# A two-layer transformer block on one core: the second layer's output projection in a new order, its splits and low parts moved

## The chip, the core and the metric

The kernel runs on one core of a Trainium2 chip. Its engines have queues of their own and wait for each other by semaphores: TensorE (PE, matrix products out of SBUF into PSUM; PEld is its weight load), VectorE (DVE), ScalarE (ACT), GpSimd (POOL) and SyncE (SP, which here issues most DMAs). Every queue is worked off in the order in which the program wrote it. The metric is the device time of one execution in microseconds, the median of several runs.

## What is computed

Two layers of a diffusion transformer on 256 latent tokens (x) and 256 context tokens, width 1024: a half FFN, an attention with three branches, a second half FFN; both halves and the attention are modulated by vectors made from a condition. In the second layer the context ends with the attention, so that all behind it is 256 tokens wide. The change concerns the lines marked by the arrows, for the second layer:

```python
def _half_ffn(h, g, shift, scale, gate, w_up, w_down):
    return h + 0.5 * gate * _swiglu(_modulate(_rmsnorm(h, g), shift, scale), w_up, w_down)
...
        o_a = _neighbourhood_attn(q_a, k_a, v_a, k_a_c, v_a_c, na_rpb[l])
        o_b = _pool_mix(p_x[..., OFF_B_U:OFF_C_Q], pool_w[l], pool_scale[l])
        o_c = _gqa_blocks(q_c, jnp.concatenate([k_c, k_c_c], axis=1), jnp.concatenate([v_c, v_c_c], axis=1))
        h_x = h_x + mod_x[:, :, 5] * (jnp.concatenate([o_a, o_b, o_c], axis=-1) @ w_out[l])      # <-
        h_x = _half_ffn(h_x, norm_g[l, 2], mod_x[:, :, 6], mod_x[:, :, 7], mod_x[:, :, 8], ffn2_up[l], ffn2_down[l])   # <-
```

## The kernel before

**Layout.** The residual stream hT lies transposed in SBUF: 8 chunks of 128 features by 512 columns, the first 256 of them x. All weights come from HBM as float32 and every product is made of three: an operand is split into a high part (rounded to the type fp32r) and a low part (the rest), and mm3 (L345) adds high x high, high x low and low x high in PSUM (L349, L350, L351; L644 to L646 in the last FFN).

**Weights.** They come as a stream in the order of use. SP loads 1 MB at a time into one of three raw buffers (loads, L167). A raw buffer is split into two slots by emit_split (L292): ACT makes the high part (L307), DVE the low part by a subtraction (L310); 128 x 1024 for each here. There are seven slot buffers, used also for attention's keys and transposed probabilities. st["out"] counts the slots that are split and not yet used up; pump (L328) splits ahead while it is under st["look"]; take hands the next slot out (and splits it, if that hasn't been done) and done gives it back and pumps. A raw buffer is free for its next load when both its splits are done.

**Order.** The program is written out by hand for each queue. A clock counted along with the matmuls (tick) fires what was put off by later(us, ...): adds, statistics, pumps.

**The stretch in question.** At the end of the second layer's attention, the last two head pairs (1 and 3 of the four of the third branch, L1010 to L1023: a product, the spread of the sums, then ACT's high part L1022 and DVE's low part L1023) are computed after all others. Then st["look"] becomes 5 at once and 6 some 6 us of the counted clock later (LOOKS), so three slots are split in a row. w_out_phase (L1198) calls proj_out (L468) for the second half of w_out, the third branch's 512 features: eight chunks of 128 output features, four steps of 128 input features each (one step a head pair). The weight is four slots of two chunks each. The first two slots are taken one after the other, with two PSUM banks each, and the steps go 0, 1, 2, 3; each slot given back lets pump split another. The last two slots are taken together and their four chunks done one by one. PSUM has five banks for such products (ps_mm).

After each chunk comes resid (L463, DVE: PSUM times the gate plus hT), then plain_operand's chunk (L610): with chunk 0 a memset and two small operations on the operand's last columns (L614, L615, L616), then for each chunk ACT's high part of hT times the norm's gain (L619) and DVE's low part (L620). Then acc_chunk (L364): ACT squares the chunk (L372, L375) and POOL adds the squares (L382), put off by 2.3 us of the counted clock. After the last chunk, after (L629) puts off the norm's statistics (stat, L404: matmuls L411, then a chain of small operations on DVE from L390 to L399) by 3.6 and the factors (L418, L625) by 6.6; a pump follows at 4.5 (REFILL).

last_ffn (L634) doesn't wait for the statistics: it multiplies the operand without the norm's factor, which is applied to the products afterwards (L662 to L675). Its product 0 needs one chunk of the operand for each of its eight steps, product 1 the same chunks with the next slot, and so on; f0, f1, f2, ... are the slots of these products. proj_out also calls ada_step (L196) after each of the first two slots, for the modulation vectors; when the second layer's projection runs, none are left to be made.

Of the kernel before, what the change touches and what calls it, by code (L numbers as in the profile page):

```python
# [18 lines left out]
TX = 256  # L19
# [7 lines left out]
RAW_BUFS = 3  # L27
NA_LOOK = (5, 5)
GQA_LOOK = (4, 3)
LOOKS = (((0, 5), (3.0, 6)), ((0, 5), (6.0, 6)))  # L30
ADAQ = lambda nc: nc.sync
ADA_AHEAD = 2
AT = ((1, 2), (0, 1), (0, 1))
# [18 lines left out]
def dit_kernel(  # L52
# [50 lines left out]
    def later(us, fn):  # L103
        pending.append([clock[0] + us, fn])
# [184 lines left out]
            return True  # L289
        return False  # L290

    def emit_split(between=None):  # L292

        if not next_main(True):
            tick(0.0)
            assert next_main(True)
        i, j = st["split"], st.get("sub", 0)
        _, src, shape, splits = stream[i]
        raw = slots[("raw", i)]
        a, b = shape  # L300
        v = raw[:, 0:a * b].rearrange("p (a b) -> p a b", a=a)
        sl = splits[j](v)
        n0, n1 = sl.shape[1], sl.shape[2]
        w = wp.tile([128, 2, 1024], F32R, tag="w", name="w")
        wh = w[:, 0, 0:n0 * n1].rearrange("p (a b) -> p a b", a=n0)
        wl = w[:, 1, 0:n0 * n1].rearrange("p (a b) -> p a b", a=n0)
        ACT.copy(out=wh, in_=sl)  # L307
        if between:
            between()
        DVE.tensor_tensor(out=wl, in0=sl, in1=wh.bitcast(F32), op=ALU.subtract)  # L310
        slots[("w", st["nslot"])] = (wh, wl)
        st["nslot"] += 1
        st["out"] += 1
        j += 1
        if j == len(splits):
            slots.pop(("raw", i))
            if i not in borrowed:
                st["raws"] -= 1
            i, j = i + 1, 0
            loads()  # L320
        st["split"], st["sub"] = i, j
# [23 lines left out]
    def mm3(ps, pairs, n, start, stop):  # L345

        last = len(pairs) - 1
        for i, ((wh, wl), (ah, al)) in enumerate(pairs):
            PE.matmul(out=ps, lhsT=wh, rhs=ah, start=start and i == 0, stop=False)  # L349
            PE.matmul(out=ps, lhsT=wh, rhs=al, start=False, stop=False)  # L350
            PE.matmul(out=ps, lhsT=wl, rhs=ah, start=False, stop=stop and i == last)  # L351
            tick(3 * MM[n])

    def wcol(slot, k, j):
        return slot[0][:, k, j * 128:(j + 1) * 128], slot[1][:, k, j * 128:(j + 1) * 128]

    def acol(a, k, lo, hi):
        return a[:, 0, k, lo:hi], a[:, 1, k, lo:hi]
# [5 lines left out]
    def acc_chunk(vs, k):  # L364

        lo, hi = vs[0] * TX, vs[-1] * TX + TX
        if k == 0:
            if 0 in vs:
                accs["sum"] = tmp.tile([128, NT], F32, tag="acc", bufs=1, name="acc")
            for v in vs:  # L370
                accs[v] = [accs["sum"][:, v * TX:v * TX + TX]]
            ACT.activation(out=accs["sum"][:, lo:hi], in_=hT[:, k, lo:hi], func=AF.Square)  # L372
            return
        sq = tmp.tile([128, NT], F32, tag="t2k", bufs=T2K, name="sq")[:, 0:hi - lo]
        ACT.activation(out=sq, in_=hT[:, k, lo:hi], func=AF.Square)  # L375
        if k == KD - 1:
            for v in vs:
                accs[v].append(sq[:, v * TX - lo:v * TX - lo + TX])
        else:
            acc = accs["sum"]  # L380
            eng = POOL if st["ends"] == 4 else DVE
            adds.append(lambda: eng.tensor_tensor(out=acc[:, lo:hi], in0=acc[:, lo:hi], in1=sq, op=ALU.add))  # L382
            later(ACC_LAG[st["ends"]], lambda: adds and adds.pop(0)())
# [77 lines left out]
    def resid(ps, k, v, gate):  # L461
        cols = slice(v * TX, v * TX + TX)
        DVE.scalar_tensor_tensor(out=hT[:, k, cols], in0=ps, scalar=gate[:, k, v:v + 1], in1=hT[:, k, cols], op0=ALU.mult, op1=ALU.add)  # L463
# [4 lines left out]
    def proj_out(src, kl, ppair, gate, both, final, after, each=None, first=None):  # L468


        n = NT if both else TX
        nsl = KD // ppair
        for i in range(nsl - 2 if final else nsl):
            s = take()
            pss = [mm_bank() for _ in range(ppair)]
            for k in range(kl):
                for j in range(ppair):
                    mm3(pss[j][:, 0:n], [(wcol(s, k, j), src(k, 0, n))], n, k == 0, k == kl - 1)
            for j in range(ppair):
                for v in halves(both):  # L480
                    resid(pss[j][:, v * TX:v * TX + TX], ppair * i + j, v, gate)
                if final:
                    if first:
                        first(ppair * i + j)
                    acc_chunk(halves(both), ppair * i + j)
                    if each:
                        each(ppair * i + j)
            done()
            ada_step()
        if not final:  # L490
            return
        sl = [take() for _ in range(2)]
        for v in halves(both):
            for i in range(2):
                for j in range(ppair):
                    ch = ppair * (nsl - 2 + i) + j
                    ps = mm_bank()
                    mm3(ps[:, 0:TX], [(wcol(sl[i], k, j), src(k, v * TX, v * TX + TX)) for k in range(kl)], TX, True, True)
                    resid(ps[:, 0:TX], ch, v, gate)
                    if first:  # L500
                        first(ch)
                    acc_chunk((v,), ch)
                    if each:
                        each(ch)
            after(v)
        st["out"] -= 2
        later(REFILL[st["ends"]], pump)
        st["ends"] += 1
# [94 lines left out]
    def plain_operand(i):  # L603


        l, n = divmod(i, 3)
        shift = modT[:, l * 72 + 3 * n * 8:l * 72 + 3 * n * 8 + 8, 0:1]
        a = {"wait": []}

        def chunk(k):  # L610
            if k == 0:
                t = actp.tile([128, 8192], F32R, tag="act", name="act")[:, 0:2 * KD * NX]
                a["t"] = t = t.rearrange("p (s k t) -> p s k t", s=2, k=KD)
                DVE.memset(t[:, :, :, TX + 1:NX].bitcast(F32), 0.0)  # L614
                ACT.copy(out=t[:, 0, :, TX:TX + 1], in_=shift)  # L615
                DVE.tensor_tensor(out=t[:, 1, :, TX:TX + 1], in0=shift, in1=t[:, 0, :, TX:TX + 1].bitcast(F32), op=ALU.subtract)  # L616
            ah, al = acol(a["t"], k, 0, TX)
            g = gsc[:, i, k, 0:1]
            ACT.activation(out=ah, in_=hT[:, k, 0:TX], func=AF.Copy, scale=g)  # L619
            DVE.scalar_tensor_tensor(out=al, in0=hT[:, k, 0:TX], scalar=g, in1=ah.bitcast(F32), op0=ALU.mult, op1=ALU.subtract)  # L620

        def factors():
            rb = spread(0)
            a["rb"] = tmp.tile([128, NT], F32, tag="acc", bufs=1, name="rb")[:, 0:TX]
            ACT.copy(out=a["rb"], in_=rb[:, 0:TX])  # L625
            while a["wait"]:
                a["wait"].pop(0)()

        def after(v):  # L629
            later(3.6, lambda: stat(0))  # L630
            later(6.6, factors)
        return a, chunk, after
# [564 lines left out]

    def w_out_phase(l, O, both, after, first=None):  # L1198
        gate = modT[:, l * 72 + 40:l * 72 + 48, :]
        proj_out(lambda k, lo, hi: acol(O, 4 + k, lo, hi), 4, 2, gate, both, True, after, None, first)  # L1200


    ada_all = [[(g, k) for k in range(KD)] for g in range(9)]
# [7 lines left out]
    with tc.manual_schedule():  # L1211
# [100 lines left out]
        def first():  # L1312

            ps = [mm_bank() for _ in range(4)]

            def dense(h, js):
                for k in (2 * h, 2 * h + 1):
                    for j in js:
                        mm3(ps[j], [(wcol(sl[j], k, 0), acol(a["t"], k, 0, NT))], NT, k == 0, k == KD - 1)
            sl = [take() for _ in range(4)]  # L1320
            for h in range(3):
                dense(h, range(0, AT[h][0]))
                sb = quarter_ada(h + 1)
                if h == 0:
                    raws.append(quarter_load(3, 1, fresh()))
                else:
                    st["raws"] -= 1
                    loads()
                dense(h, range(AT[h][0], AT[h][1]))
                quarter_finish(h + 1, sb)  # L1330
                dense(h, range(AT[h][1], 4))
            st["raws"] -= 1
            loads()
            for i in range(2):
                dense(3, (2 * i, 2 * i + 1))
                done(2)
            return ps
# [117 lines left out]
```

## Time and profile before

| | us |
|---|---|
| runs | 1714.87, 1713.21, 1712.35 |
| median | 1713.21 |
| profiled execution | 1716.47 |
| its span | 1714.7 |

The span is the time between the first and the last instruction of the profiled execution; durations and starts below are counted from its beginning. A time in the profile is of that one execution, not of the median. The kernel's line numbers are those in the profile: "PE mm L349" is the matmul of line 349. For the stretch in question one reads the waits of an engine (who waited for whom, us in total, times, longest), the order of time of each engine (start, duration, what ran, in brackets the idle time before it and what ended it), and stretches of equal length with each engine's busy time and the clock granted to PE. Where instructions with the same text follow each other, a row merges them and gives their count.

### The profile page before, as it was taken

What the parts mean: (1) busy time and instruction counts of PE and PEld (TensorE: products, weight loads), DVE (VectorE), ACT (ScalarE), POOL (GpSimd) and SP (SyncE); (2) the same over time, 40 slices, a digit from 0 to 9 for tenths busy, and PEclk for the clock granted to TensorE, in tenths of its full rate; (3) what the DMA queues carried; (4) which work ended last, traced back from release to release, by engine and by line L of the source; (5) the groups of instructions that cost most, each with busy time, mean ns of one, the idle gap of its engine ahead of it and who ended that gap; (6) DMA issues with size and microseconds to landing.
All of it is one profiled execution on the core that took longest, in us unless ns stands there. A gap on an engine that the chain in (4) does not pass through costs nothing.

```text
span 1714.7 us, 23726 instructions
## 1 busy us (share of the span) xinstructions
PE 1679.2 (98%) x9512; PEld 1421.6 (83%) x9512; DVE 1037.6 (61%) x1782; ACT 670.8 (39%) x1135; POOL 43.6 (3%) x66
## 2 busy tenths in 40 slices
PE   6999999999999999999999999999999999999998
PEld 4778888889886798888888898888888987789998
DVE  4666577667555676666764466545433656676674
ACT  4432222334556644222233243213222356654443
POOL 0000200000010000000000000020000000000000
PEclk8999999999999999999999999999999999999999
DMA  9745556431304325554553335455532234555561
GB/s 314 203 165 174 166 164 190 163 131 51 111 25 172 108 72 177 172 154 136 172 171 118 98 87 182 145 155 174 151 99 88 66 111 148 172 172 175 169 199 50
DMA packets 295335, 246.48 MB, mean 144 GB/s; under 512 B 9377, under 2 KB 262442, under 8 KB 293176
## 3 DMA queue, kind: packets, MB, share of 16 engines
q1 hardware_dynamic: 292680, 241.30, 45.5%
q0 software_dynamic: 1088, 2.15, 0.5%
q8 instruction: 75, 1.23, 0.3%
q10 hardware_dynamic: 1456, 1.52, 0.3%
q14 instruction: 36, 0.29, 0.1%
HBM read 243.88 MB, written 2.00 MB: 143 GB/s over the span
## 4 chain that ended last, share of the span: by engine, by line
PE 89%; DVE 4%; DMA 3%; ACT 2%; issue 1%; SPq 0%; DVEq 0%; ACTq 0%
PE mm L349 25%; PE mm L350 24%; PE mm L351 24%; PE mm L644 2%; PE mm L645 2%; PE mm L646 2%; PE mm L1010 1%; DVE w L310 1%; PE aux L976 1%; DMA ada_raw<-in_w_ada_dram 1%; PE ada L182 1%; PE mm L936 1%; DVE ada_acc L222 1%; PE mm L937 1%; PE ada L230 1%
## 5 line engine op out<-in xcount | busy, mean ns | idle before, releaser
L349 PE MATMUL mm<-act,w 128*128 128x512 f32 (+1 forms) x2240 | 810.8, 362 | 4.5 <-ACT act L1022 2.2
L350 PE MATMUL mm<-act,w 128*128 128x512 f32 (+1 forms) x2240 | 804.0, 359 | 1.1 <-DVE act L433 0.9
L351 PE MATMUL mm<-act,w 128*128 128x512 f32 (+1 forms) x2240 | 803.3, 359 | 1.7 <-DVE w L310 1.7
L310 DVE TENSOR_TENSOR w<-raw,w 128x1024 fp32r<-128x1024 f32 (+1 forms) x312 | 371.3, 1199 | 220.2 <-ACT w L307 219.2
L349 PEld LDWEIGHTS mm<-act,w 128*128 128x128 f32 x2240 | 424.9, 190 | 86.0 <-issue 15.9
L351 PEld LDWEIGHTS mm<-act,w 128*128 128x128 f32 x2240 | 424.8, 190 | 64.6 <-DVE w L310 2.5
L350 PEld LDWEIGHTS mm<-act,w 128*128 128x128 f32 x2240 | 425.0, 190 | 62.9 <-DVE act L433 1.4
L307 ACT CAST w<-raw 128x1024 fp32r<-128x1024 f32 (+1 forms) x312 | 315.4, 1025 | 119.9 <-PE mm L351 92.7
L222 DVE SCALAR_TENSOR_TENSOR ada_acc<-ada_raw,sc,ada_acc 128x512 f32<-128x512 f32 x308 | 216.2, 747 | 51.2 <-DMA ada_raw<-in_w_ada_dram 27.2
L564 ACT CAST act<-gf 128x512 fp32r<-128x512 f32 x66 | 41.0, 621 | 278.7 <-DVE gf L561 278.7
L463 DVE SCALAR_TENSOR_TENSOR hT<-mm,hgt,hT 128x256 f32<-128x256 f32 x168 | 75.1, 480 | 95.7 <-PE mm L351 95.2
L558 ACT ACTIVATE sil<-mm 128x512 f32<-128x512 f32 x66 | 39.4, 596 | 183.2 <-PE mm L351 183.1
L644 PE MATMUL mm<-act,w 128*128 128x258 f32 x352 | 101.3, 288 | 3.7 <-ACT act L619 3.3
L645 PE MATMUL mm<-act,w 128*128 128x258 f32 x352 | 100.9, 287 | 0.1
L646 PE MATMUL mm<-act,w 128*128 128x258 f32 x352 | 100.1, 284 | 0.0
L561 DVE TENSOR_TENSOR gf<-sil,mm 128x512 f32<-128x512 f32 x66 | 45.4, 687 | 80.7 <-PE mm L351 70.1
L565 DVE TENSOR_TENSOR act<-gf,act 128x512 fp32r<-128x512 f32 x66 | 45.7, 692 | 45.4 <-ACT act L564 45.4
L644 PEld LDWEIGHTS mm<-act,w 128*128 128x128 f32 x352 | 67.2, 191 | 4.9 <-ACT act L619 4.8
L645 PEld LDWEIGHTS mm<-act,w 128*128 128x128 f32 x352 | 67.6, 192 | 1.0 <-DVE act L620 1.0
L646 PEld LDWEIGHTS mm<-act,w 128*128 128x128 f32 x352 | 67.3, 191 | 0.0
L375 ACT ACTIVATE sq<-hT 128x256 f32<-128x256 f32 (+1 forms) x52 | 25.5, 489 | 102.5 <-DVE hT L463 102.4
L439 ACT ACTIVATE act<-nt,modT 128x256 fp32r<-128x256 f32 x80 | 39.5, 507 | 41.3 <-DVE nt L438 41.2
(170 smaller groups left out, 1158.3 us busy)
## 6 DMA issues: line engine op xcount, KB each, us to landing
raw<-in_ffn_up_dram SPq DMA_DIRECT2D x172, 512.0 KB
ada_raw<-in_w_ada_dram SPq DMA_DIRECT2D x192, 256.0 KB
raw<-in_ffn_down_dram SPq DMA_DIRECT2D x32, 1024.0 KB
raw<-in_w_ada_dram SPq DMA_DIRECT2D x16, 1024.0 KB
raw<-in_ffn_down_dram SPq DMA_DIRECT2D x16, 768.0 KB
raw<-in_w_in_dram SPq DMA_DIRECT2D x10, 1024.0 KB
raw<-in_w_out_dram SPq DMA_DIRECT2D x8, 1024.0 KB
raw<-in_w_ada_dram SPq DMA_DIRECT2D x12, 512.0 KB
```

The source lines that it names most:

```text
L222: DVE.scalar_tensor_tensor(out=o, in0=raw, scalar=col, in1=o, op0=ALU.mult, op1=ALU.add)
L307: ACT.copy(out=wh, in_=sl)
L310: DVE.tensor_tensor(out=wl, in0=sl, in1=wh.bitcast(F32), op=ALU.subtract)
L349: PE.matmul(out=ps, lhsT=wh, rhs=ah, start=start and i == 0, stop=False)
L350: PE.matmul(out=ps, lhsT=wh, rhs=al, start=False, stop=False)
L351: PE.matmul(out=ps, lhsT=wl, rhs=ah, start=False, stop=stop and i == last)
L463: DVE.scalar_tensor_tensor(out=hT[:, k, cols], in0=ps, scalar=gate[:, k, v:v + 1], in1=hT[:, k, cols], op0=ALU.mult, op1=ALU.add)
L561: DVE.tensor_tensor(out=u[:, 0:n], in0=s[:, 0:n], in1=pb[:, 0:n], op=ALU.mult)
L565: DVE.tensor_tensor(out=gl, in0=uv, in1=gh.bitcast(F32), op=ALU.subtract)
L644: PE.matmul(out=ps[:, 0:NX], lhsT=wh, rhs=ah, start=k == 0, stop=False)
L645: PE.matmul(out=ps[:, 0:NX], lhsT=wh, rhs=al, start=False, stop=False)
L646: PE.matmul(out=ps[:, 0:NX], lhsT=wl, rhs=ah, start=False, stop=k == KD - 1)
```

## The change

For the second layer alone, w_out_phase no longer calls proj_out.

- The two lookahead steps become one: st["look"] is 5 after the attention and not raised to 6; instead one more slot is split by hand before the projection, its subtraction on POOL. With the two that the attention left, six slots are split ahead: the four of w_out, and f0 and f1.
- st["look"] is 0 during the projection, so none is split among the chunks. After the last chunk it is 3, and 6 after a further 4.5 us of the counted clock.
- The first two slots are taken together, with four PSUM banks; step by step over all four chunks, with the head pairs in the order 0, 2, 1, 3. Then the other two slots, two chunks each, chunk after chunk in the same order of pairs.
- chunk returns the low part (L620) as a function: it is issued after the next chunk's residual, the last one after all chunks. ACT's parts, the squares and POOL's adds keep their order.
- ada_step is not called there.

```diff
-LOOKS = (((0, 5), (3.0, 6)), ((0, 5), (6.0, 6)))
+LOOKS = (((0, 5), (3.0, 6)), ((0, 5),))
...
-    def emit_split(between=None):
+    def emit_split(between=None, eng=DVE):
...
-        DVE.tensor_tensor(out=wl, in0=sl, in1=wh.bitcast(F32), op=ALU.subtract)
+        eng.tensor_tensor(out=wl, in0=sl, in1=wh.bitcast(F32), op=ALU.subtract)
...
-            DVE.scalar_tensor_tensor(out=al, in0=hT[:, k, 0:TX], scalar=g, in1=ah.bitcast(F32), op0=ALU.mult, op1=ALU.subtract)
+            return lambda: DVE.scalar_tensor_tensor(out=al, in0=hT[:, k, 0:TX], scalar=g, in1=ah.bitcast(F32), op0=ALU.mult, op1=ALU.subtract)
...
     def w_out_phase(l, O, both, after, first=None):
         gate = modT[:, l * 72 + 40:l * 72 + 48, :]
-        proj_out(lambda k, lo, hi: acol(O, 4 + k, lo, hi), 4, 2, gate, both, True, after, None, first)
+        if both:
+            proj_out(lambda k, lo, hi: acol(O, 4 + k, lo, hi), 4, 2, gate, both, True, after)
+            return
+
+        emit_split(eng=POOL)
+        st["look"] = 0
+        lows = []
+
+        def finished(ps, ch):
+            resid(ps[:, 0:TX], ch, 0, gate)
+            lows.append(first(ch))
+            if ch:
+                lows.pop(0)()
+            acc_chunk((0,), ch)
+
+        def product(ps, s, k, j, n):
+            mm3(ps[:, 0:TX], [(wcol(s, k, j), acol(O, 4 + k, 0, TX))], TX, n == 0, n == 3)
+        order = (0, 2, 1, 3)
+        sl = [take() for _ in range(2)]
+        pss = [mm_bank() for _ in range(4)]
+        for n, k in enumerate(order):
+            for ch in range(4):
+                product(pss[ch], sl[ch // 2], k, ch % 2, n)
+        for ch in range(4):
+            finished(pss[ch], ch)
+        for i in range(2):
+            s = take()
+            for j in range(2):
+                ps = mm_bank()
+                for n, k in enumerate(order):
+                    product(ps, s, k, j, n)
+                finished(ps, 4 + 2 * i + j)
+        lows.pop(0)()
+        after(0)
+        st["out"] -= 4
+        st["look"] = 3
+        pump()
+
+        def refill():
+            st["look"] = W_BUFS - 1
+            pump()
+        later(REFILL[st["ends"]], refill)
+        st["ends"] += 1
```

## The prediction

> **What bounds the kernel now.** First the page's busy shares, then the waits of TensorE (PE) in the stretch of the second layer's output projection (1480 to 1520 us) and in all that follows.
>
> ```profile
> span 1714.7 us, 23726 instructions
> PE 1679.2 (98%) x9512; PEld 1421.6 (83%) x9512; DVE 1037.6 (61%) x1782; ACT 670.8 (39%) x1135; POOL 43.6 (3%) x66
> ...
> PE mm L644 <- ACT act L619: 3.3, 1, 3.3
> PE mm L349 <- ACT act L1022: 1.7, 1, 1.7
> ...
> PE aux L411 <- DVE acc L382: 0.9, 1, 0.9
> ```
>
> PE is the bound, 98% busy. The first two waits lie where the change is made; the third is the only one from 1520 to the end. So what PE gains by 1520 reaches the end, unless something new makes it wait later. More than 3.3 + 1.7 us is lost there, as PE's order of time shows (start, duration, then the wait in brackets); the last two lines are stretches of 3.41 us with the busy time of PE, weight loads, DVE, ACT and POOL, then the granted clock, 0.50, the DMA share and GB/s:
>
> ```profile
> 1489.84 0.36 PE L349 MATMUL mm<-act,w 128*128 128x256 f32 x1
> ...
> 1490.15 0.28 PE L351 MATMUL mm<-act,w 128*128 128x256 f32 x1
> 1490.27 0.28 PE L349 MATMUL mm<-act,w 128*128 128x256 f32 x1
> ...
> 1492.45 0.38 PE L349 MATMUL mm<-act,w 128*128 128x256 f32 x1 [1.66 <-ACT act L1022]
> ...
> 1503.72 0.28 PE L351 MATMUL mm<-act,w 128*128 128x256 f32 x1
> 1503.85 0.36 PE L644 MATMUL mm<-act,w 128*128 128x258 f32 x1
> ...
> 1508.87 0.39 PE L644 MATMUL mm<-act,w 128*128 128x258 f32 x1 [3.32 <-ACT act L619]
> ...
> 1516.56 0.50 PE L411 MATMUL aux<-ones,acc 128*128 128x1 f32 x4
> ...
> 1509.24:1512.65 3.41, 3.00 (x8) 1.91 (x8) 2.25 (x6) 1.63 (x4) 1.92 (x3) 0.50 1.06 291
> 1512.65:1516.07 3.42, 3.28 (x13) 2.75 (x13) 2.09 (x4) 3.38 (x5) 0.27 (x1) 0.50 0.05 12
> ```
>
> From the first projection matmul (1489.84) to the norm's statistics (L411, 1516.56) pass 26.7 us. The work in them is 8 chunks x 4 steps x 3 = 96 matmuls and 36 of the last FFN (all eight steps of product 0, four of product 1), 0.12 apart: 15.8 us. So 10.9 are lost: the two waits, smaller ones as the operand trickles in, and the half clock. Why the operand is late stands in the order of time of DVE and ACT:
>
> ```profile
> 1490.31 0.42 DVE L1019 TENSOR_TENSOR rec<-mm,rec 128x256 f32<-128x256 f32 x1 [3.11 <-ACT rec L1018]
> 1492.43 0.43 DVE L1023 TENSOR_TENSOR act<-rec,act 128x256 fp32r<-128x256 f32 x1 [0.47 <-ACT act L1022]
> 1493.38 3.50 DVE L310 TENSOR_TENSOR w<-raw,w 128x1024 fp32r<-128x1024 f32 x3 [0.52 <-ACT w L307]
> 1496.80 0.48 DVE L463 SCALAR_TENSOR_TENSOR hT<-mm,modT,hT 128x256 f32<-128x256 f32 x1
> 1497.21 0.15 DVE L616 TENSOR_TENSOR act<-modT,act 128x8 fp32r<-128x8 f32 x1
> ...
> 1505.52 2.36 DVE L310 TENSOR_TENSOR w<-raw,w 128x1024 fp32r<-128x1024 f32 x2 [0.76 <-ACT w L307]
> 1507.80 0.48 DVE L463 SCALAR_TENSOR_TENSOR hT<-mm,modT,hT 128x256 f32<-128x256 f32 x1
> 1508.86 0.48 DVE L620 SCALAR_TENSOR_TENSOR act<-hT,gsc,act 128x256 fp32r<-128x256 f32 x1 [0.58 <-ACT act L619]
> 1509.26 0.48 DVE L463 SCALAR_TENSOR_TENSOR hT<-mm,modT,hT 128x256 f32<-128x256 f32 x1
> ...
> 1492.31 2.94 ACT L307 CAST w<-raw 128x1024 fp32r<-128x1024 f32 x3
> 1497.31 0.51 ACT L619 ACTIVATE act<-hT,gsc 128x256 fp32r<-128x256 f32 x1 [1.96 <-DVE act L614]
> 1497.72 0.40 ACT L372 ACTIVATE acc<-hT 128x256 f32<-128x256 f32 x1
> ```
>
> Two things: splits (L310) stand among the residuals, here until 1507.80; and the turn residual (L463), ACT's high part (L619), low part (L620), next residual is serial, 1509.26 - 1507.80 = 1.46 a chunk.
>
> **The change part by part.** Times are of the profiled execution.
>
> *Head pairs 0 and 2 first, four chunks at once.* 24 matmuls need no late operand: 1489.84 + 24 x 0.12 = 1492.72. The late pair's low part is there at 1492.43 + 0.43 = 1492.86, so 0.1 is waited in place of 1.66. The fourth chunk needs a fourth PSUM bank; L1019 frees one at 1490.73, and PE asks for it at 1489.84 + 9 x 0.12 = 1490.92. Chunk 0 is complete at 1494.8, chunk 3 at 1495.8. By itself this gains nothing: DVE's three splits still end at 1496.88, and residual 0 stays at 1496.8. Were it the other L1019's bank, 1.2 us later, chunk 0 would still be in time.
>
> *Sixth split, its subtraction on POOL.* ACT's fourth high part ends at 1492.31 + 2.94 + 0.95 = 1496.2, ahead of its next work (1497.31). A subtraction of that size on POOL is not in the trace; the nearest rows:
>
> ```profile
> 1387.39 1.32 POOL L838 TENSOR_TENSOR qkv<-qkv,rope 128x256 f32<-128x256 f32 x1 [32.60 <-PE aux L834]
> 1386.89 2.90 DVE L310 TENSOR_TENSOR w<-raw,w 128x1024 fp32r<-128x1024 f32 x2 [1.12 <-ACT w L307]
> ...
> 1509.27 0.73 POOL L382 TENSOR_TENSOR acc<-acc,sq 128x256 f32<-128x256 f32 x1 [3.84 <-ACT sq L375]
> 1420.93 1.29 POOL L838 TENSOR_TENSOR qkv<-qkv,rope 128x512 f32<-128x512 f32 x1 [9.56 <-PE aux L834]
> ```
>
> Beside a POOL product of 256 columns two DVE splits take 2.90 against 2.36, 0.54 more, and the product 1.32 against 0.73 for the add of its size: each waits out the other. POOL's 256 columns thus hold DVE for about 0.53; 1024 hold it for 4 x 0.53 = 2.13 (by 0.73 and 1.29 the whole operation is 0.73 + 3 x 0.56 = 2.4). The residual at 1509.26, with one input in PSUM, ran beside POOL's add undisturbed, 0.48. So I let POOL and those DVE operations exclude each other that have two SBUF inputs: the splits, L616 and the low parts. POOL's turn begins as the third split ends, 1496.83, and lasts to 1498.96. Residual 0 passes, L616 is held, and behind it DVE's whole queue: 1.7 us.
>
> The Trainium skill, "SBUF — State Buffer", section "SBUF: two separate sides", states such a lock, between GpSimd and DVE operations with two SBUF inputs, held for the whole instruction. The rows on splits agree; for L616 and the low parts no row shows it.
>
> *Residuals ahead of low parts, no splits among the chunks.* Residual k+1 fills the time in which ACT makes high part k. DVE's cost per chunk, bounded: 0.41 + 0.41 = 0.82 if POOL's add (0.53) disturbs nothing; 0.41 + 0.53 = 0.94 if it shuts out low parts; 0.41 + 0.41 + 0.53 = 1.35 if residuals too. ACT's 0.41 + 0.31 is less. I take 0.94, by the rows above, from residual 4 on; the adds are not there before. Residual 1 starts at 1499.06, 3 at 1500.70, 7 at 1500.70 + 4 x 0.94 = 1504.46. Low part 6 from 1505.0, POOL's last add 1505.4 to 1505.94, then low part 7, there at 1506.43.
>
> PE meanwhile: chunk 4 from 1495.8, chunks 5, 6 and 7 wait for the banks of residuals 0, 1 and 2 (1497.3, 1499.55, 1500.4); the last is complete at 1502.6. Product 0 begins at 1502.5, waits for its steps 4 to 7, and ends two matmuls after low part 7: product 1 starts at 1506.7, the statistics at 1506.7 + 12 x 0.12 = 1508.2. **Sum: 1516.56 - 1508.2 = 8.4 us earlier.** The half clock goes with the gap of 3.32.
>
> *Splits put off behind the chunks.* In hand are f0 and f1 (POOL, 1499.1); f2's subtraction ends at 1508.0 and is used at 1508.2 + 0.8 (L411) + 12 x 0.12 + 0.25 = 1510.7. f3 follows by 1509.2 for 1513.6. f4 to f6 stand behind the statistics' chain:
>
> ```profile
> 1517.88 0.15 DVE L390 TENSOR_SCALAR rs_v<-aux 128x2 f32<-128x2 f32 x1
> ...
> 1519.82 0.16 DVE L399 SCALAR_TENSOR_TENSOR rs_y<-rs_t,rs_y 128x2 f32<-128x2 f32 x1
> ...
> 1501.88 0.99 SPq L151 DMA_DIRECT2D raw<-in_ffn_up_dram  x2
> 1507.91 0.99 SPq L151 DMA_DIRECT2D raw<-in_ffn_up_dram  x2
> 1505.83:1509.24 3.41, 0.37 (x1) 0.19 (x1) 2.83 (x4) 1.42 (x3) 0.00 (x0) 1.00 0.35 83
> 1382.95:1386.36 3.41, 2.21 (x20) 2.12 (x19) 1.24 (x3) 2.92 (x8) 0.00 (x0) 1.00 0.00 0
> 1386.36:1389.77 3.41, 2.94 (x11) 2.23 (x11) 2.88 (x3) 3.41 (x5) 1.32 (x1) 0.50 0.09 24
> ```
>
> The chain takes 2.1 us, from 1509.2 to 1511.3, so f4 is there at 1512.5 for 1516.5: hidden by 4 us. SP's loads follow the splits: the raw of f0 and f1 is free at 1499.1 (1501.88 before), the next with f3's split at 1509.2, later than 1507.91. It feeds slot f8, used some 18 us later, while a load issued at 1507.91 kept the DMA engines busy to about 1512.7. The adaptive-step calls that fall away in this phase issued nothing. Cost of all this: nothing, and the same PE order to the end.
>
> **The rivals.** 1. *No exclusion for small operations and the chain at 0.82*: residual 0 frees chunk 5's bank at 1497.3, three chunks of 1.44 end at 1501.7, 36 matmuls later come the statistics, 1506.1: 10.4 earlier. For it: nothing shows L616 or a low part held. 2. *More exclusion*: residuals shut out too, 3 x (0.94 - 0.82) + 4 x (1.35 - 0.94) = 2.0 more, or the POOL operation twice as long, 2.1 more: 6.3 to 6.4 earlier. 3. *The clock halves after all*: PE is starved in a stretch of 3.41 us and then gets 6.83 us of half clock (two stretches, as from 1509.24), losing 3.4: 5.0 earlier. For it, the stretch at 1382.95 with 2.21 busy was followed by 0.50, not only the empty one at 1505.83 (0.37). Against it, product 0 has seven of its steps, 21 matmuls, in the stretch from 1502.4. The Trainium skill, "TensorE: Matmul & The Clock Gate", section "Part 1", drops the clock after an idle window of about 3.4 us; by that this rival falls away, though 2.21 us busy is not idle. 4. *The gain is handed back*: three slots in hand, not six, and PE waits for weights until it stands where it did: no change. It needs f4 12 us late (4 + 8.4); only loads could be. 5. *Slower*: POOL's subtraction with its fp32r output is not in the trace. If it took t, L616 and thus all of DVE would wait: the gain is 8.4 - (t - 2.13), gone at t = 10.5; at 15 the kernel is 4.5 us slower. The adds' 0.73 speaks against it.
>
> **How the numbers follow.** The profiled run took 1716.47 us, 1.8 of it around the span, and is 3.3 above the median of 1713.21; I take the gain off the median: 1713.2 - 8.4 = 1704.8. The rivals give 1702.8, 1706.9, 1708.2, 1713.2 and 1717.7. Chances: forecast 0.46, rivals 0.22, 0.12, 0.07, 0.08, 0.05. The range takes in the first four and a us of the runs' scatter: 1701.5 to 1708.7. Under 0.2%, 3.4 us, a measurement can't tell from no change. Faster 0.87, same 0.08, slower 0.05.
>
> **What would show it.** Right: PE's wait of 3.32 and the half clock around 1510 gone; L411 near 1508; POOL's split near 2.3 us with L616 or the low part behind it stretched or late; low parts 0.94 apart; no PE wait after 1520 but the 0.9. Wrong: low parts 0.82 apart and L616 at 1497.3 (rival 1); new waits of L351 or L646 for L310 (4), or of anything for POOL's L310 (5).

## The result, and the profile after

| | before | changed |
|---|---|---|
| median of 4 runs, us | 1714.04 | 1704.74 |
| lowest and highest | 1712.35, 1716.38 | 1703.69, 1705.38 |
| profiled execution, and its span | 1716.47, 1714.7 | 1705.38, 1703.6 |

The ratio of the runs is 0.9945 with a 95% interval of 0.9933 to 0.9957: about 9.4 us faster, between 7.4 and 11.5. Forecast was 1704.8.

The waits of PE in the stretch (1480 to 1515 us of the changed kernel's profile), then its order of time. The rows of before that answer to them are those with 1.66 and 3.32 us.

```profile
PE mm L349 <- DVE hT L463: 0.7, 1, 0.7
PE aux L247 <- ACT PT L984: 0.2, 1, 0.2
PE mm L645 <- DVE act L620: 0.2, 1, 0.2
```

```profile
1487.43 0.36 PE L349 MATMUL mm<-act,w 128*128 128x256 f32 x1
...
1490.52 0.39 PE L350 MATMUL mm<-act,w 128*128 128x256 f32 x1
...
1497.31 0.36 PE L349 MATMUL mm<-act,w 128*128 128x256 f32 x1 [0.68 <-DVE hT L463]
...
1500.25 0.28 PE L644 MATMUL mm<-act,w 128*128 128x258 f32 x1
...
1503.68 0.38 PE L645 MATMUL mm<-act,w 128*128 128x258 f32 x1 [0.24 <-DVE act L620]
...
1505.45 0.50 PE L411 MATMUL aux<-ones,acc 128*128 128x1 f32 x4
```

From the first projection matmul to the statistics pass 1505.45 - 1487.43 = 18.02 us, where 26.72 passed before: **8.70 us** are gained in the stretch. It is the measure used below; it leaves out what happened earlier in the same execution. Behind it nothing was lost or gained: from L411 to the end of the span 198.1 us in both. The spans differ by 11.1. The other 2.4 lie ahead of the stretch, in code that is the same: there it began at 1489.84 before and begins at 1487.43 here. The granted clock differs there between the executions; one such place is the same work around 438 us, which ran at half clock in the profile of before (first row) and at full clock in that of the changed kernel (second row; the clock is the third number from the end). One matmul there starts at 438.02 before and 436.75 here, one a little later at 440.51 and 438.10, so this place makes 1.1 of the 2.4. The medians, 9.3 apart, are the better measure of the whole.

```profile
437.46:440.87 3.41, 3.41 (x9) 2.72 (x10) 2.74 (x2) 3.41 (x4) 1.19 (x1) 0.50 0.05 12
```

```profile
436.00:439.40 3.40, 3.40 (x17) 2.91 (x18) 2.28 (x3) 3.40 (x5) 1.69 (x1) 1.00 0.00 0
```

The order of time of DVE, and of POOL, in the stretch of the changed kernel, and the last of its stretches of 3.41 us before the statistics:

```profile
1490.98 3.50 DVE L310 TENSOR_TENSOR w<-raw,w 128x1024 fp32r<-128x1024 f32 x3 [0.52 <-ACT w L307]
1494.39 0.48 DVE L463 SCALAR_TENSOR_TENSOR hT<-mm,modT,hT 128x256 f32<-128x256 f32 x1
1494.81 1.96 DVE L616 TENSOR_TENSOR act<-modT,act 128x8 fp32r<-128x8 f32 x1
...
1496.69 0.47 DVE L463 SCALAR_TENSOR_TENSOR hT<-mm,modT,hT 128x256 f32<-128x256 f32 x1
1497.08 0.47 DVE L620 SCALAR_TENSOR_TENSOR act<-hT,gsc,act 128x256 fp32r<-128x256 f32 x1
...
1498.26 0.47 DVE L463 SCALAR_TENSOR_TENSOR hT<-mm,modT,hT 128x256 f32<-128x256 f32 x1
1498.66 0.57 DVE L620 SCALAR_TENSOR_TENSOR act<-hT,gsc,act 128x256 fp32r<-128x256 f32 x1
...
1501.79 0.47 DVE L463 SCALAR_TENSOR_TENSOR hT<-mm,modT,hT 128x256 f32<-128x256 f32 x1
1502.19 1.44 DVE L620 SCALAR_TENSOR_TENSOR act<-hT,gsc,act 128x256 fp32r<-128x256 f32 x2
```

```profile
1493.87 2.86 POOL L310 TENSOR_TENSOR w<-raw,w 128x1024 fp32r<-128x1024 f32 x1 [65.85 <-ACT w L307]
1498.15 5.19 POOL L382 TENSOR_TENSOR acc<-acc,sq 128x256 f32<-128x256 f32 x6 [1.42 <-ACT sq L375]
```

```profile
1502.41:1505.83 3.42, 3.07 (x25) 2.66 (x23) 2.87 (x4) 3.42 (x5) 0.85 (x2) 1.00 0.00 0
```

None of the stretches of 3.41 us from 1485.35 to 1522.89 shows less than 1.00. DVE waits for nothing from 1490.98 to the end of the last low part, 1502.19 + 1.44 = 1503.63, or 16.2 of the stretch. Before, the last low part ended 23.9 after the first projection matmul:

```profile
1513.23 0.49 DVE L620 SCALAR_TENSOR_TENSOR act<-hT,gsc,act 128x256 fp32r<-128x256 f32 x1 [0.58 <-ACT act L619]
```

The one operation that grew is L616: eight columns, 0.15 us before and 1.96 here, for as long as POOL's subtraction ran.

### The profile page after: what moved, and what is told of

The parts are those of the page before. It is cut to its first block, busy times and chain, and to the rows that moved or that the text cites. A ratio compares the mean times of both kernels' runs of the same rounds, so it can differ in the third digit from the quotient of the medians.

```text
span 1703.6 us, 23729 instructions
## 1 busy us (share of the span) xinstructions
PE 1672.7 (98%) x9512; PEld 1417.9 (83%) x9512; DVE 1037.6 (61%) x1781; ACT 670.7 (39%) x1135; POOL 47.6 (3%) x67
## 4 chain that ended last, share of the span: by engine, by line
PE 90%; DVE 4%; DMA 3%; ACT 2%; issue 1%; SPq 0%; DVEq 0%; ACTq 0%
PE mm L349 25%; PE mm L350 25%; PE mm L351 25%; PE mm L645 2%; PE mm L644 2%; PE mm L646 2%; PE mm L1010 1%; PE aux L976 1%; DMA ada_raw<-in_w_ada_dram 1%; DVE w L310 1%; PE ada L182 1%; PE mm L936 1%; DVE ada_acc L222 1%; PE mm L937 1%; PE ada L230 1%
## 5 line engine op out<-in xcount | busy, mean ns | idle before, releaser
L463 DVE SCALAR_TENSOR_TENSOR hT<-mm,hgt,hT 128x256 f32<-128x256 f32 x168 | 75.1, 480 | 95.9 <-PE mm L351 95.6
L645 PE MATMUL mm<-act,w 128*128 128x258 f32 x352 | 99.5, 283 | 0.3 <-DVE act L620 0.2
L644 PE MATMUL mm<-act,w 128*128 128x258 f32 x352 | 99.8, 284 | 0.0
L646 PE MATMUL mm<-act,w 128*128 128x258 f32 x352 | 99.3, 282 | 0.0
```

The lines of the kernel that those rows point to most:

```text
L644: PE.matmul(out=ps[:, 0:NX], lhsT=wh, rhs=ah, start=k == 0, stop=False)
L645: PE.matmul(out=ps[:, 0:NX], lhsT=wh, rhs=al, start=False, stop=False)
L646: PE.matmul(out=ps[:, 0:NX], lhsT=wl, rhs=ah, start=False, stop=k == KD - 1)
```

## The experiments

All times of stretches are from the first projection matmul to the statistics, of one profile each. "Total" is the median, with the ratio to the kernel before run on the same chip.

| kernel | stretch | less than before | total | ratio, 95% interval |
|---|---|---|---|---|
| before | 26.72 | | | |
| changed | 18.02 | 8.70 | 1704.74 | 0.9945, 0.9933 to 0.9957 |
| e1_order | 18.04 | 8.68 | 1704.5 | 0.9940, 0.9921 to 0.9958 |
| e7_two_order | 18.18 | 8.54 | 1705.14 | 0.9943, 0.9925 to 0.9961 |
| e2_low_now | 23.19 | 3.53 | 1710.06 | 0.9983, 0.9973 to 0.9992 |
| e3_splits_among | 23.67 | 3.05 | 1712.0 | 0.9988, 0.9979 to 0.9997 |
| e4_dve | 17.55 | 9.17 | 1703.75 | 0.9941, 0.9926 to 0.9956 |
| e5_pool_twice | 19.93 | 6.79 | 1705.23 | 0.9946, 0.9928 to 0.9964 |
| e8_late | 17.07 | 9.65 | 1702.18 | 0.9932, 0.9917 to 0.9948 |
| e9_late_p1 | 16.18 | 10.54 | 1703.68 | 0.9937, 0.9921 to 0.9953 |
| c1_changed | 18.02 | 8.70 | 1704.62 | 0.9951, 0.9939 to 0.9964 |
| c2_late_p1 | 16.18 | 10.54 | 1702.75 | 0.9945, 0.9931 to 0.9959 |

The totals of one kernel scatter by some 2 us; the stretch came out the same to 0.01 in both repeats (c1 repeats the changed kernel, c2 repeats e9). What differs by less than 2 us is therefore read from the stretch. Where a half clock falls into it (before, e2, e3) there is one profile of each, so how much its place varies isn't shown.

In all kernels but e9 and c2 the stretch holds the same 132 matmuls, and from L411 to the end of the span pass 198.10 to 198.13 us, so nothing is handed back later. In e9 and c2 L411 comes two matmuls sooner in PE's order: the stretch holds 130, and 198.35 us follow. To compare these two with the rest, 0.24 us have to be added to their stretch: 16.42, and 10.30 less than before.

### The order of the head pairs, and two slots together

e1:

```diff
-        order = (0, 2, 1, 3)
+        order = (0, 1, 2, 3)
```

> The changed kernel with the head pairs in their old order 0, 1, 2, 3; all else as changed. The stretch from the first projection matmul to the statistics (L411) is 18.0 us in the changed kernel, 26.7 before. My theory: DVE's chain decides, and it can't start before its three splits end, so PE waits 1 to 1.3 us for the late pair after 12 matmuls and makes it up before residual 0: stretch 18.0 to 18.3. Rival (the wait of 1.66 for the late pair is part of the gain): 19.0 to 19.7.

e7, the same and:

```diff
-        sl = [take() for _ in range(2)]
-        pss = [mm_bank() for _ in range(4)]
-        for n, k in enumerate(order):
-            for ch in range(4):
-                product(pss[ch], sl[ch // 2], k, ch % 2, n)
-        for ch in range(4):
-            finished(pss[ch], ch)
+        for i in range(2):
+            s = take()
+            pss = [mm_bank() for _ in range(2)]
+            for n, k in enumerate(order):
+                for j in range(2):
+                    product(pss[j], s, k, j, n)
+            for j in range(2):
+                finished(pss[j], 2 * i + j)
```

> The changed kernel with the first two slots taken one after the other (two chunks, two banks each) and the head pairs in the order 0, 1, 2, 3, as before; splits, low parts and lookahead as changed. My theory: worth nothing while DVE's splits end after chunk 0: stretch 18.0 to 18.2. Rival (PE's wait of 1.66 and the two chunks' later end count): 19.0 to 19.7.

PE's waits in the stretch, e1 first, then e7:

```profile
PE mm L349 <- ACT act L1022: 0.9, 1, 0.9
PE mm L645 <- DVE act L620: 0.2, 1, 0.2
```

```profile
PE mm L349 <- ACT act L1022: 1.7, 1, 1.7
```

The wait for the late pair is back, 0.9 us and with e7 the whole 1.7, and the stretch is 0.02 and 0.16 longer. The part of the change that stands first in its name is worth 0.02 to 0.16 us here: what PE saves at the start it waits for later, because residual 0 stands behind DVE's three splits in any case.

### Low parts behind the next residual

e2, each low part at once, as before:

```diff
             lows.append(first(ch))
-            if ch:
-                lows.pop(0)()
+            lows.pop(0)()
...
-        lows.pop(0)()
         after(0)
```

> The changed kernel with each low part issued at once after its high part, ahead of the next residual, as before; no splits among the chunks. My theory: the serial turn of 1.46 us a chunk is back, stretch 18.0 + 3.8 = 21.8, total 3.8 us over the changed kernel. Rival (the gain is that of the splits alone): stretch 18.0 to 18.5.

DVE's order of time in e2, and two of its stretches:

```profile
1496.15 0.48 DVE L463 SCALAR_TENSOR_TENSOR hT<-mm,modT,hT 128x256 f32<-128x256 f32 x1
1497.21 0.49 DVE L620 SCALAR_TENSOR_TENSOR act<-hT,gsc,act 128x256 fp32r<-128x256 f32 x1 [0.58 <-ACT act L619]
1497.61 0.47 DVE L463 SCALAR_TENSOR_TENSOR hT<-mm,modT,hT 128x256 f32<-128x256 f32 x1
...
1504.49 0.49 DVE L620 SCALAR_TENSOR_TENSOR act<-hT,gsc,act 128x256 fp32r<-128x256 f32 x1 [0.58 <-ACT act L619]
```

```profile
1501.64:1505.05 3.41, 2.14 (x8) 1.13 (x8) 2.18 (x5) 2.13 (x6) 1.46 (x2) 0.98 0.00 0
1505.05:1508.46 3.41, 3.41 (x17) 3.41 (x17) 2.36 (x2) 3.41 (x5) 0.00 (x0) 0.52 0.00 0
```

The turn is 1.46 us a chunk again, with 0.58 of waiting for ACT in each. The last low part ends at 1504.98, 19.97 after the first projection matmul (which was at 1485.01): 3.8 later than in the changed kernel, as expected. The stretch grew by 5.2, not 3.8. The other 1.4 are the clock: PE, starved, was busy for 2.14 of 3.41 us and got half the clock in the next 3.4, and the 14 matmuls from the last low part to L411 took 3.2 us where they took 1.8 in the changed kernel.

### Splits among the chunks

e3:

```diff
-LOOKS = (((0, 5), (3.0, 6)), ((0, 5),))
+LOOKS = (((0, 5), (3.0, 6)), ((0, 5), (6.0, 6)))
...
-        emit_split(eng=POOL)
-        st["look"] = 0
...
         for ch in range(4):
             finished(pss[ch], ch)
+            if ch % 2:
+                done()
...
         after(0)
-        st["out"] -= 4
-        st["look"] = 3
-        pump()
-
-        def refill():
-            st["look"] = W_BUFS - 1
-            pump()
-        later(REFILL[st["ends"]], refill)
+        st["out"] -= 2
+        later(REFILL[st["ends"]], pump)
```

> The changed kernel with the splits back among the chunks, on DVE (one after chunk 1, two after chunk 3 or 4, the lookahead raised to 6 as before, no sixth split ahead), low parts still behind the next residual. My theory: three splits of 1.15 us stand in DVE's full queue, less what the POOL split cost: stretch 18.0 + 3.0 = 21.0. Rival (DVE has room for them once the low parts are deferred): 18.0 to 19.0.

DVE's order of time in e3, a wait of PE, and a stretch of 3 us:

```profile
1497.19 0.48 DVE L620 SCALAR_TENSOR_TENSOR act<-hT,gsc,act 128x256 fp32r<-128x256 f32 x1
1499.14 1.23 DVE L310 TENSOR_TENSOR w<-raw,w 128x1024 fp32r<-128x1024 f32 x1 [1.47 <-ACT w L307]
...
1503.37 2.36 DVE L310 TENSOR_TENSOR w<-raw,w 128x1024 fp32r<-128x1024 f32 x2 [1.44 <-ACT w L307]
```

```profile
PE mm L645 <- DVE act L620: 2.9, 1, 2.9
```

```profile
1506.00:1509.00 3.00, 2.43 (x9) 2.15 (x9) 3.00 (x8) 2.78 (x7) 1.73 (x3) 0.50 0.67 192
```

The stretch is 5.65 longer than the changed kernel's, not 3.0. A split in DVE's queue costs more than its 1.15: it stands ahead of the next low part and waits for ACT's cast, which itself stands behind the chunk's high part and square. DVE idles 1.47 us before the first and 1.44 before the next two. The last low part ends at 1509.92, 20.75 of the stretch, 4.6 later than in the changed kernel; the other 1.1 go with the half clock that follows PE's wait of 2.9.

e2 alone gains 3.5 us over the kernel before and e3 alone 3.1; both edits together gain 8.7. Together they are worth 2.1 us more than the sum. About 0.6 of that lies in the chain: its last low part ends 3.9 and 3.1 us earlier with one edit, 7.7 with both. The other 1.5 lie behind it, where each alone still starves PE long enough to get half the clock: from the last low part to the statistics pass 2.8 us before, 3.2 in e2, 2.9 in e3 and 1.8 in the changed kernel.

### POOL's split

e4, on DVE:

```diff
-        emit_split(eng=POOL)
+        emit_split()
```

> The changed kernel with the sixth split's subtraction on DVE, not POOL. My theory: POOL's operation holds DVE for 1.9 us at L616 anyway, a DVE split takes 1.15: stretch 18.0 - 0.5 = 17.5, total equal or 0.5 less. Rival (POOL relieves DVE of a split): stretch 18.0 + 1.2 = 19.2.

DVE's order of time in e4:

```profile
1489.53 4.63 DVE L310 TENSOR_TENSOR w<-raw,w 128x1024 fp32r<-128x1024 f32 x4 [0.52 <-ACT w L307]
1494.08 0.48 DVE L463 SCALAR_TENSOR_TENSOR hT<-mm,modT,hT 128x256 f32<-128x256 f32 x1
1494.50 0.15 DVE L616 TENSOR_TENSOR act<-modT,act 128x8 fp32r<-128x8 f32 x1
```

Four splits in a row take 4.63, L616 its 0.15 again, and the stretch is 0.47 shorter than with POOL. POOL doesn't relieve DVE here: it holds DVE longer than the split would take.

e5, POOL's subtraction done twice:

```diff
-        eng.tensor_tensor(out=wl, in0=sl, in1=wh.bitcast(F32), op=ALU.subtract)
+        for _ in range(2 if eng is POOL else 1):
+            eng.tensor_tensor(out=wl, in0=sl, in1=wh.bitcast(F32), op=ALU.subtract)
```

> The changed kernel with POOL's subtraction of the sixth split done twice in a row (the same result twice). My theory: the second one starts before DVE gets its turn or right after L616, and holds DVE's two-input operations for another 2.2 us, since residual and low parts stand behind: stretch (first projection matmul to L411) 18.0 + 2.2 = 20.2, less by what POOL's gap between the two lets through; if DVE takes the turn between the two, L616 and residual 1 pass and low part 0 is held, about 0.4 less: 19.8. Rival (POOL's work lies beside DVE's, its cost is nothing): 18.0 to 18.2.

POOL and DVE in e5 (its lines are one further down: L617 is L616, L464 is L463, L621 is L620):

```profile
1493.09 5.31 POOL L311 TENSOR_TENSOR w<-raw,w 128x1024 fp32r<-128x1024 f32 x2 [65.84 <-ACT w L307]
```

```profile
1494.03 1.94 DVE L617 TENSOR_TENSOR act<-modT,act 128x8 fp32r<-128x8 f32 x1
...
1495.90 0.47 DVE L464 SCALAR_TENSOR_TENSOR hT<-mm,modT,hT 128x256 f32<-128x256 f32 x1
1496.29 2.39 DVE L621 SCALAR_TENSOR_TENSOR act<-hT,gsc,act 128x256 fp32r<-128x256 f32 x1
```

The second subtraction holds low part 0 for 2.39 in place of 0.47, and the stretch grows by 1.91. Residual 1, with one input in PSUM, runs through beside POOL in its usual 0.47, as the residuals of the changed kernel do beside POOL's adds. So the exclusion here is between POOL and DVE operations with two SBUF inputs; it is seen with 8 columns (L616) and with 256 (low part 0).

### A version that beats both

e8: the sixth split's high part stays where it is; its subtraction goes to DVE behind the last low part.

```diff
-        emit_split(eng=POOL)
+        held = []
+        emit_split(put=held)
...
         lows.pop(0)()
+        for fn in held:
+            fn()
         after(0)
```

where emit_split(put=...) puts the subtraction, and the release of the raw buffer, into that list. e9 (and c2) also does product 1 in two passes:

```diff
+            if late:
+                for k in range(KD):
+                    wh, wl = wcol(s, k, 0)
+                    ah, al = acol(t, k, 0, NX)
+                    PE.matmul(out=ps[:, 0:NX], lhsT=wh, rhs=ah, start=k == 0, stop=False)
+                    PE.matmul(out=ps[:, 0:NX], lhsT=wh, rhs=al, start=False, stop=False)
+                    tick(2 * MM[TX])
+                for k in range(KD):
+                    PE.matmul(out=ps[:, 0:NX], lhsT=wcol(s, k, 0)[1], rhs=acol(t, k, 0, NX)[0], start=False, stop=k == KD - 1)
+                    tick(MM[TX])
+                return
```

> The changed kernel with the sixth split's high part where it is and its subtraction on DVE behind the last low part, none on POOL. My theory: the chain of chunks starts without the 1.9 us at L616 and ends 1.7 us earlier, at 14.5 of the stretch; slot f1 is then ready at 15.7 and PE waits for it 0.6 in product 1: stretch 17.0, total about 1 us under the changed kernel. Rival (PE waits for f1 as long as DVE is ahead): 18.0.

> As e8_late, and product 1 does its 16 matmuls with the slot's high part first, then the 8 with the low part, so that the late subtraction has 1.9 us more. My theory: PE runs on behind low part 7: stretch 16.4 to 16.6, total about 1.5 us under the changed kernel. Rival: as e8_late, 17.0.

> The changed kernel again, on the same chip as the next, as its base: stretch 18.0, 8 to 9.5 us under the kernel before in the median.

> The sixth split's subtraction on DVE behind the last low part and product 1 in two passes (as e9_late_p1), beside the changed kernel: stretch 16.2, and since PE waits for nothing new behind it, 1.8 us less in the median. Rival (its gain of the stretch is given back later, in f1 to f6 or in the products): within 0.5 us of the changed kernel, with PE waits between 1505 and 1530.

PE's only wait of note in e8's stretch (L656 is the product's third matmul), and the only one of c2 from 1483 to 1700 us (L421 is L411, at the very end):

```profile
PE mm L656 <- DVE w L310: 0.4, 1, 0.4
```

```profile
PE aux L421 <- DVE acc L392: 0.9, 1, 0.9
```

e8 takes 0.95 off the stretch, which still has a wait of 0.4 for slot f1 in it (0.6 was expected). e9 takes that wait away too: 16.18, where its 130 matmuls alone are 15.6. With the 0.24 us that it leaves behind L411 it is 16.42, the lower end of what was expected, and 1.60 less than the changed kernel, not 1.84: from the first projection matmul to the end of the span pass 214.53 us in c2 and 216.12 in c1. The two ran on the same chip, with medians of 1702.75 and 1704.62, 1.9 apart. By their intervals the totals alone would not tell them apart.

## Why the prediction was right

**The bound.** PE stayed the bound, and what the stretch gained came out at the end: 198.1 us from L411 to the end of the span, before and after.

**Head pairs 0 and 2 first: nothing by itself.** Right. PE waited 0.1 (the row at 1490.52), and e1 and e7, without this part, lose 0.02 and 0.16.

**The sixth split on POOL: 2.13 us of hold, 1.7 of it lost.** Right. POOL's row runs from its start behind the cast, 1493.87, to 1496.73; DVE's third split ended at 1494.47, so about 2.3 us are POOL's own. L616 took 1.96, 1.8 more than before. The reading of two overlapping rows (2.90 against 2.36) gave the price of an operation four times as long. That it came out so close by the number of columns is partly luck: POOL's rows before had no more than 512. The first rival, no exclusion for small operations, falls with L616, and e5 shows the hold for a low part as well. The second rival falls with the residual in e5, and with the 2.3 us, where it needed twice the 2.13. What the Trainium skill says in "SBUF — State Buffer", section "SBUF: two separate sides", that such a lock is kept for the whole instruction, agrees with eight columns that waited 1.8 us.

**Cadence 0.94 with POOL's adds.** Right in kind, a little off in size: residuals 1498.26 to 1501.79 are four chunks, 0.88 each. A low part beside an add takes 0.57 for 0.47, and starts while the add is under way; the adds start 0.88 apart and take 0.80 each, for 0.73 before. I had let the add hold the low part for its full 0.53. That term, 4 x 0.06 = 0.2, is most of the difference between the 8.4 forecast for the stretch and the 8.70 measured.

**PE beside it.** Forecast, shifted by the 2.41 us by which this execution was ahead: product 0 from 1500.1, statistics at 1505.8. Measured: 1500.25 and 1505.45. The bank wait that was foreseen is the 0.68 for residual 1.

**The half clock.** It went, as forecast (1.00 throughout). The third rival was a real danger, though: in e2 and e3, where PE is starved less than before, it came back and cost 1.1 to 1.4 us.

**Splits behind the chunks.** Hidden, as forecast: no PE wait from 1515 on but the 0.9 at the end that was there before. The fourth and fifth rivals didn't come.

**The total.** 8.4 off the median of 1713.21 gave 1704.8; the measured 1704.74 is closer than the method deserves, since the runs scatter by a us or two and the medians are 9.3 apart.

## What to carry to other kernels

When a queue is in the way of the bounding engine, look first at what stands in it between two operations that depend on each other through a third engine: putting the independent one of the next turn in that gap, and the work that nobody waits for behind the whole chain, was worth 8.7 us here, while the reordering of the bounding engine's own work was worth 0.16 us at most. Moving an operation to GpSimd didn't take it off VectorE here, since the VectorE operations beside it read two inputs from SBUF; an 8-column operation was the one that paid (1.96 us for 0.15). To compare variants that differ by less than the runs scatter, measure the stretch between two instructions of the profile, and count that it holds the same work in each: in e9 it didn't.

## What the runs showed of the hardware

A gap needn't be empty for TensorE to lose its clock. In e2 PE was busy for 2.14 of 3.41 us, by short bursts of three matmuls, and the next 3.4 us ran at 0.52. Busy time alone doesn't decide: in the kernel before, a stretch with 2.03 us busy was followed by full clock.

```profile
1488.76:1492.17 3.41, 2.03 (x18) 1.36 (x14) 1.19 (x3) 1.22 (x4) 0.00 (x0) 1.00 0.62 162
1492.17:1495.59 3.42, 3.06 (x23) 2.86 (x24) 2.63 (x3) 3.18 (x5) 0.00 (x0) 1.00 0.02 5
```

The Trainium skill, "TensorE: Matmul & The Clock Gate", section "Part 1: The HAM clock gate", speaks of an idle window of about 3.4 us; the length agrees with the rows of e2, idle does not. The eight matmuls in that window weren't enough; where the line lies, the runs don't settle.
